# Mixer B: one of four chunks of the depth by seven block products instead of eight, in six pairs of projection column blocks

## The chip, the cores and the metric

The kernel runs on one core of a Trainium2 chip. The time is the device time of one execution in microseconds (us); less is better. Three runs of the kernel before gave 2266.64, 2268.15 and 2270.43 us, with a median of 2268.15 us. A core has five engines that work side by side: PE (TensorE, the matrix multiplier; the loading of its weights is shown as PEld), DVE (VectorE), ACT (ScalarE), POOL (GpSimd) and SP, whose queue starts most transfers. Each takes its own instructions strictly in the order in which they were written into its queue.

## The reference, cut to what matters

A trunk of two layers over 256 positions of width 2048, all in float32: attention A and a gated MLP, then attention B (mixer B) and a second gated MLP. The change is in mixer B:

```python
def mixer_b(h, w_qkv, w_o, rel_bias):
    qkv = (h @ w_qkv).reshape(b, s, 3, 3, 8, 128)     # groups g, q/k/v, heads
    for g, (window, dil) in enumerate(((128, 1), (512, 4), (2048, 16))):
        o, lz = dilated_group(qkv[:, :, g, 0], qkv[:, :, g, 1], qkv[:, :, g, 2], ...)
    wts = jax.nn.softmax(jnp.stack(log_zs, axis=0), axis=0)
    y = jnp.concatenate([wts[g][..., None] * outs[g] for g in range(3)], axis=2)
    return y.reshape(b, s, 3072) @ w_o
```

The product that matters is `h @ w_qkv`: 256 positions, a depth of 2048, and 9216 columns.

## The kernel before, in words

**One float32 product is three passes.** A weight block is loaded to SBUF (tile `raw`, 128 x 1024, which is 256 rows of depth by 512 columns, 512 KB), ACT copies it to a rounded tile `wh`, and DVE writes the rest `raw - wh` into `wl` (`split_raw`, L125). The positions are split in the same way into `xh` and `xl`. A product is then xh·wh, xh·wl and xl·wh, summed in a PSUM bank. For one block PE does 12 matmuls of 128 x 512: three passes, two halves of the depth, two halves `m` of the positions. Such a block of 12 matmuls is called a full block below.

**Rings.** `raw` has six buffers (`new_raw`), and `wh`/`wl` have three (`new_hl`; a fourth only in the down projections of the MLP). So the split of a block waits until PE has finished the block three before it. A split is issued with a priority (AHEAD = 45) that puts it ahead of other work in the queues of ACT and DVE.

**Mixer B** (`mixer_b`, L917) takes the heads in two halves `hf`. In each half it projects nine column blocks of 512 one after another: k and q of group 0, k and q of group 1, k and q of group 2, then v of groups 0, 1 and 2. A projection (`project`, L180) goes through four chunks `kg` of the depth with two full blocks each, so eight full blocks. It accumulates in two of the PSUM banks 0 to 3, and the next projection takes the other two. Banks 4 to 7 rotate through `ps_tile` and hold the small products of the attention.

**What runs beside the projections.** After a projection a generator is started: `k_gen` and `s_gen` copy the result from PSUM with a scale (L686, ACT), transpose 32 x 32 blocks (L335, DVE), and put the blocks in their places with 16 copies of 32 x 256 (L345 to L349: 12 on ACT, 4 on POOL). This gives kT and qT. Then `s_gen` makes the scores of four heads on PE (L305 for groups 1 and 2, L307 to L309 for group 0), adds the bias and takes the maximum (L975, L977, DVE) and the exponential (L986, ACT). A score matmul needs all 16 copies of qT. `v_gen` scales the probabilities (L1014, DVE), transposes them on PE (L1016), and multiplies them with v. `step()` moves the oldest waiting generator forward by one `yield`; it is called after each weight block. So the number of blocks between the end of a projection and a step of its generator is set by the code, and a scheduler then lays the instructions down in each engine's queue.

**Seven products.** The down projections of the MLP use `project_pair` (L215) already: two column blocks n0 and n1 are done together, and on chosen chunks the 2 x 2 x 2 block products (depth halves, position halves, column blocks) are done by seven instead of eight. A product P takes 6 matmuls, needs sums of positions (`forms`) and sums of weight blocks, which DVE adds in place in `raw` (L242), and leaves common terms M1, M5, M6 and M7 that are added to the four results afterwards (`combine`).

## Time and profile before

| | |
|---|---|
| median of three runs | 2268.15 us |
| the profiled execution | 2266.05 us, of which the span on the core is 2264.2 us |
| PE busy | 2248.7 us (99%) |
| DVE busy | 1635.8 us (72%) |
| ACT busy | 1504.0 us (66%) |
| mean granted TensorE clock | 0.998 |

The profile shows one execution. Times in it are counted from the start of the span. The end of a matmul in it is modelled, so that neighbouring matmuls overlap in the rows; the distance from start to start is what a matmul takes on PE. The projections of mixer B lie from 983.6 to about 1398 us; one projection with the attention work between its matmuls takes about 23 us.

### The profile page before, as it was taken

What the parts mean: (1) busy time and instruction counts of PE and PEld (TensorE: products, weight loads), DVE (VectorE), ACT (ScalarE), POOL (GpSimd) and SP (SyncE); (2) the same over time, 40 slices, a digit from 0 to 9 for tenths busy, and PEclk for the clock granted to TensorE, in tenths of its full rate; (3) what the DMA queues carried; (4) which work ended last, traced back from release to release, by engine and by line L of the source; (5) the groups of instructions that cost most, each with busy time, mean ns of one, the idle gap of its engine ahead of it and who ended that gap; (6) DMA issues with size and microseconds to landing.
All of it is one profiled execution on the core that took longest, in us unless ns stands there. A gap on an engine that the chain in (4) does not pass through costs nothing.

```text
span 2264.2 us, 28877 instructions
## 1 busy us (share of the span) xinstructions
PE 2248.7 (99%) x10169; PEld 1861.7 (82%) x10169; DVE 1635.8 (72%) x2213; ACT 1504.0 (66%) x2330; POOL 252.8 (11%) x372
## 2 busy tenths in 40 slices
PE   9999999999999999999999999999999999999998
PEld 7788888888888888888888888888888888888886
DVE  6776687888878778756565556465888788687784
ACT  6665776777547777767755774565777755577763
POOL 2210112200001010111100100000101100001110
PEclk9999999999999999999999999999999999999999
DMA  8444667756665655666555565566666656556763
GB/s 299 156 149 150 193 197 227 224 190 192 210 202 189 198 189 187 219 206 205 190 172 177 177 194 161 181 193 189 198 191 194 205 184 218 187 192 195 223 198 128
DMA packets 126449, 437.42 MB, mean 193 GB/s; under 512 B 17264, under 2 KB 18032, under 8 KB 126304
## 3 DMA queue, kind: packets, MB, share of 16 engines
q1 hardware_dynamic: 119744, 425.64, 58.2%
q0 software_dynamic: 6128, 9.38, 1.6%
q8 instruction: 79, 1.29, 0.2%
q10 hardware_dynamic: 432, 0.56, 0.1%
q14 instruction: 66, 0.54, 0.1%
HBM read 429.20 MB, written 6.29 MB: 192 GB/s over the span
## 4 chain that ended last, share of the span: by engine, by line
PE 96%; ACT 1%; DVE 1%; issue 1%; DMA 1%; POOL 0%; SPq 0%; POOLq 0%; DVEq 0%; ACTq 0%
PE acc L154 26%; PE acc L155 26%; PE acc L153 26%; PE acc L273 5%; PE acc L275 5%; PE acc L278 5%; PE ps L305 1%; PE ps L309 1%; PE ps L308 1%; PE ps L307 0%; DVE wl L129 0%; PE ps L868 0%; ACT tM L347 0%; ACT wh L128 0%; PE ps L1016 0%
## 5 line engine op out<-in xcount | busy, mean ns | idle before, releaser
L129 DVE TENSOR_TENSOR wl<-raw,wh 128x1024 fp32r<-128x1024 f32 x822 | 1009.0, 1233 | 478.2 <-ACT wh L128 475.8
L128 ACT ACTIVATE wh<-raw 128x1024 fp32r<-128x1024 f32 x822 | 867.3, 1058 | 550.1 <-PE acc L155 338.6
L153 PE MATMUL acc<-wh,xh 128*128 128x512 f32 x2176 | 851.9, 392 | 0.2 <-ACT wh L164 0.2
L154 PE MATMUL acc<-wl,xh 128*128 128x512 f32 x2176 | 848.4, 390 | 2.9 <-DVE wl L129 1.4
L155 PE MATMUL acc<-wh,xh 128*128 128x512 f32 x2176 | 847.5, 389 | 0.0
L154 PEld LDWEIGHTS acc<-wl,xh 128*128 128x128 f32 x2176 | 408.7, 188 | 89.9 <-DVE wl L129 5.5
L155 PEld LDWEIGHTS acc<-wh,xh 128*128 128x128 f32 x2176 | 408.5, 188 | 84.8
L153 PEld LDWEIGHTS acc<-wh,xh 128*128 128x128 f32 x2176 | 408.7, 188 | 83.4 <-ACT wh L164 0.6
L345 POOL COPY u<-t 32x256 f32<-32x256 f32 x176 | 110.7, 629 | 1039.9 <-DVE t L455 1031.8
L273 PE MATMUL acc<-wh,ah 128*128 128x512 f32 x524 | 204.1, 389 | 0.3 <-DVE h L408 0.3
L275 PE MATMUL acc<-wh,al 128*128 128x512 f32 x524 | 203.9, 389 | 0.0
L154 PE MATMUL acc<-wl,ah 128*128 128x512 f32 x480 | 187.0, 390 | 0.5 <-DVE wl L129 0.5
L153 PE MATMUL acc<-wh,ah 128*128 128x512 f32 x480 | 187.4, 390 | 0.0
L155 PE MATMUL acc<-wh,al 128*128 128x512 f32 x480 | 186.9, 389 | 0.0
L347 ACT ACTIVATE u<-t 32x256 f32<-32x256 f32 x352 | 147.8, 420 | 12.5 <-DVE t L455 4.6
L278 PE MATMUL acc<-wl,ah 128*128 128x512 f32 x524 | 146.0, 389 | 0.0
L273 PEld LDWEIGHTS acc<-wh,ah 128*128 128x128 f32 x524 | 98.4, 188 | 21.3 <-DVE h L408 1.0
L278 PEld LDWEIGHTS acc<-wl,ah 128*128 128x128 f32 x524 | 98.4, 188 | 20.4
L275 PEld LDWEIGHTS acc<-wh,al 128*128 128x128 f32 x524 | 98.4, 188 | 20.3
L154 PEld LDWEIGHTS acc<-wl,ah 128*128 128x128 f32 x480 | 90.2, 188 | 19.3 <-DVE wl L129 0.9
L155 PEld LDWEIGHTS acc<-wh,al 128*128 128x128 f32 x480 | 90.1, 188 | 18.7
L153 PEld LDWEIGHTS acc<-wh,ah 128*128 128x128 f32 x480 | 90.2, 188 | 18.1
(180 smaller groups left out, 1641.6 us busy)
## 6 DMA issues: line engine op xcount, KB each, us to landing
raw<-in_w_up_dram SPq DMA_DIRECT2D x352, 512.0 KB, 4.4
raw<-in_w_down_dram SPq DMA_DIRECT2D x176, 512.0 KB, 4.7
raw<-in_w_b_dram SPq DMA_DIRECT2D x144, 512.0 KB, 4.1
raw<-in_w_bo_dram SPq DMA_DIRECT2D x48, 512.0 KB, 4.1
raw<-in_w_a_dram SPq DMA_DIRECT2D x40, 512.0 KB, 4.7
raw<-in_w_ao_dram SPq DMA_DIRECT2D x32, 512.0 KB, 4.0
raw<-in_w_a_dram SPq DMA_DIRECT2D x16, 256.0 KB, 6.2
h<-in_x_dram SPq DMA_DIRECT2D x4, 512.0 KB, 8.9
```

Source lines behind the costliest of these rows:

```text
L128: nc.scalar.activation(wh, r, AF.Copy)
L129: nc.vector.tensor_tensor(wl, r, wh.bitcast(F32), ALU.subtract)
L153: nc.tensor.matmul(accs[m], xh, wh[:, j, :], start=st, stop=False)
L154: nc.tensor.matmul(accs[m], xh, wl[:, j, :], start=False, stop=False)
L155: nc.tensor.matmul(accs[m], xl, wh[:, j, :], start=False, stop=sp)
L273: nc.tensor.matmul(acc[k], xh, wh[:, j, :], start=k in fresh, stop=False)
L275: nc.tensor.matmul(acc[k], xl, wh[:, j, :], start=False, stop=False)
L278: nc.tensor.matmul(acc[k], xh, wl[:, j, :], start=False, stop=last[k] == i and j == 1)
L305: nc.tensor.matmul(o, lh[ls], rh[rs], start=start, stop=stop)
L308: nc.tensor.matmul(o, lh[ls], rl[rs], start=False, stop=False)
L345: nc.gpsimd.tensor_copy(dst, src)
L347: nc.scalar.activation(dst, src, AF.Copy)
```

## The change

In each half of the heads, k and q of group 0 are projected as before. The other projections, but for v of group 2, are taken in pairs through `project_pair`: k and q of group 1, k and q of group 2, and v of group 0 with v of group 1. That makes six pairs in all. In each pair the chunks 0 to 2 are 12 full blocks ("c", 12 matmuls each), and chunk 3 is done by seven products ("P", 6 matmuls each) where it was four full blocks (eight products). The order in a pair, by the list `units` of `seven`, is c P1 c P2 c c P5 c P3 c c P7 c P6 c P4 c c c. The first six c belong to the first column block, the last six to the second. The first block is complete after P4, the second three full blocks later.

The four results of a pair hold all four PSUM banks 0 to 3. M1, M5, M7 and M6 go through the rotating banks 4 to 7. ACT copies M1, M5 and M7 into SBUF (L1110), and DVE works out the four sums (L1112 to L1115). The results are then added to them in SBUF by DVE (L1118, L1119 for the first block, L1128, L1129 for the second), and k_gen, s_gen and v_gen read them from there. In each pair ACT and DVE split 19 blocks in place of 16, and DVE adds four pairs of weight blocks (L245). The sums of positions for chunk 3 are made once, by `last_forms`, at the end of the first MLP.

```diff
-    def project_pair(w, n0, n1, lhs, forms, units, late, early_done, n0_done):
+    def project_pair(w, n0, n1, lhs, forms, units, late, early_done, n0_done, product_done=None):
         home = {1: "M1", 2: "C11", 3: "C12", 4: "C21", 5: "M5", 6: "M6", 7: "M7"}
-        place = ("M1", "M5", "M6", "M7", "C11", "C21", "C12", "C22")
-        b = bank_at[0]
-        acc = {k: bank((4, 5, 6, 7, 2 - b, 3 - b, b, b + 1)[i], "acc") for i, k in enumerate(place)}
+        if product_done:
+            acc = dict(zip(("C11", "C21", "C12", "C22"), new_acc() + new_acc()))
+        else:
+            place = ("M1", "M5", "M6", "M7", "C11", "C21", "C12", "C22")
+            b = bank_at[0]
+            acc = {k: bank((4, 5, 6, 7, 2 - b, 3 - b, b, b + 1)[i], "acc") for i, k in enumerate(place)}
 
...
+            for k, *_ in todo:
+                if k not in acc:
+                    acc[k] = ps_tile()
...
+            if product_done and kind == "P" and home[p][0] == "M":
+                product_done(home[p], acc.pop(home[p]))
             if i == last_s:
                 early_done(acc)
-            if i == last["C21"]:
+            if i == max(last["C11"], last["C21"]):
                 n0_done(acc)
...
+    def last_forms(hT, turn_pair, n, g):
+        fm = hT["forms"] = {f: new_hT(4 * n + i)[:2] for i, f in enumerate((1, 0, 2, 4))}
+        for i, f in enumerate((7, 5, 6, 3)):
+            fm[f] = tuple(hpool.tile([P, NT], F32R, tag=f"al{k}", name=nm("sf")) for k in
+                          ((12, 13), (14, 15), (20, 21), (22, 23))[i])
+        for kt in range(4):
+            hT[4 * n + kt] = [tuple(t[:, kt % 2 * P:(kt % 2 + 1) * P] for t in fm[f])
+                              for f in ((1, 0), (2, 4))[kt // 2]]
+
+        def scaled(kp):
+            t = turn_pair(kp)
+            for j in range(2):
+                kt = 4 * n + 2 * kp + j
+                nc.scalar.activation(t[:, j * NT:(j + 1) * NT], t[:, j * NT:(j + 1) * NT], AF.Copy,
+                                     scale=gain[:, g, kt:kt + 1])
+            return t.rearrange("p (a t) -> p a t", a=2)
+
+        def put(f, src):
+            split(*(t.rearrange("p (a t) -> p a t", a=2) for t in fm[f]), src)
+
+        def tmp(k):
+            return hpool.tile([P, NT], F32, tag=f"ah{k}", name=nm("st")).rearrange("p (a t) -> p a t", a=2)
+
+        c0 = scaled(0)
+        put(1, c0[:, :, :P])
+        put(0, c0[:, :, P:])
+        yield
+        c1 = scaled(1)
+        put(2, c1[:, :, :P])
+        put(4, c1[:, :, P:])
+        x0, s1, s2, s3, s4 = (tmp(k) for k in (12, 13, 14, 15, 20))
+        yield
+        nc.scalar.activation(x0, c0[:, :, P:], AF.Copy)
+        nc.vector.tensor_tensor(s3, c0[:, :, :P], x0, ALU.subtract)
+        nc.vector.tensor_tensor(s1, c1[:, :, P:], x0, ALU.subtract)
+        put(7, s3)
+        put(5, s1)
+        yield
+        nc.vector.scalar_tensor_tensor(s2, s1, -1.0, c0[:, :, :P], ALU.mult, ALU.subtract)
+        nc.vector.tensor_tensor(s4, c1[:, :, :P], s2, ALU.add)
+        put(6, s2)
+        put(3, s4)
...
+                kTs = {}
+
+                def k_gen(g, accs, kTs=kTs):
                     ks = evac_scaled(bp, accs, rstd)
                     yield
                     yield
+                    kT = kTs[g] = pair_tile(bp, [P, 4, NT], "kT", 1, g > 0)
                     yield from heads_T_dve(kT, ks, bp, "vl")
 
-                def s_gen(g, accs, kT, bts, nmx=nmx, lsum=lsum, nmv=nmv, probs=probs, e=e):
+                def s_gen(g, accs, bts, nmx=nmx, lsum=lsum, nmv=nmv, probs=probs, e=e, kTs=kTs):
                     qs = evac_scaled(bp, accs, rstd)
-                    qT = pair_tile(bp, [P, 4, NT], "qT", 1, g > 0)
-                    yield
-                    yield
+                    yield
+                    yield
+                    kT, qT = kTs[g], pair_tile(bp, [P, 4, NT], "qT", 1, g > 0)
                     yield from heads_T_dve(qT, qs, bp, "vl")
...
                 def v_gen(g, accs, hf=hf, probs=probs, e=e):
+                    if g > 0:
+                        yield
                     v = evac_split(bp, accs, rstd, g > 0)
...
+                def seven(n0, n1, sums, n0_ready, n1_ready):
+                    (k0, k1), (q0, q1) = sums
+                    chores = []
+
+                    def product_done(k, t):
+                        if k != "M6":
+                            nc.scalar.activation({"M1": k0, "M5": q1, "M7": k1}[k], t, AF.Copy)
+                            return
+                        nc.vector.tensor_tensor(q0, t, k0, ALU.add)
+                        nc.vector.tensor_tensor(k1, k1, q0, ALU.add)
+                        nc.vector.tensor_tensor(q0, q0, q1, ALU.add)
+                        nc.vector.tensor_tensor(q1, k1, q1, ALU.add)
+
+                    def n0_done(a):
+                        nc.vector.tensor_tensor(k0, a["C11"], k0, ALU.add)
+                        nc.vector.tensor_tensor(k1, a["C21"], k1, ALU.add)
+                        n0_ready([k0, k1])
+
+                    cs = [("c", k, i) for i2 in range(2) for k in kgs[:3] for i in (2 * i2, 2 * i2 + 1)]
+                    units = [cs.pop(0)]
+                    for p, c in zip(ORDER, (1, 2, 1, 2, 1, 1, 3)):
+                        units += [("P", 3, p)] + [cs.pop(0) for _ in range(c)]
+                    a = project_pair(w_b, n0, n1, hT, {3: hT["forms"]}, units, None, lambda a: None,
+                                     n0_done, product_done)
+                    nc.vector.tensor_tensor(q0, a["C12"], q0, ALU.subtract)
+                    nc.vector.tensor_tensor(q1, a["C22"], q1, ALU.subtract)
+                    n1_ready([q0, q1])
+
                 for g in range(3):
                     bts = biases(hf, g)
-                    ka = project(w_b, 6 * g + 2 + hf, hT, kgs)
-                    kT = pair_tile(bp, [P, 4, NT], "kT", 1, g > 0)
-                    start(k_gen(ka, kT))
-                    start(s_gen(g, project(w_b, 6 * g + hf, hT, kgs), kT, bts))
-                for g in range(3):
-                    start(v_gen(g, project(w_b, 6 * g + 4 + hf, hT, kgs)))
+                    n0, n1 = 6 * g + 2 + hf, 6 * g + hf
+                    if g == 0:
+                        start(k_gen(g, project(w_b, n0, hT, kgs)))
+                        start(s_gen(g, project(w_b, n1, hT, kgs), bts))
+                    else:
+                        sums = [[bp.tile([P, 512], F32, tag=t, name=nm("ms"), bufs=2) for _ in range(2)]
+                                for t in ("pTh", "pTl")]
+                        seven(n0, n1, sums, lambda a: start(k_gen(g, a)), lambda a: start(s_gen(g, a, bts)))
+                sums = [(lambda t: [t[:, 0], t[:, 1]])(bp.tile([P, 2, 512], F32, tag=t, name=nm("ms"), bufs=1))
+                        for t in ("kTl", "qTl")]
+                seven(4 + hf, 10 + hf, sums, lambda a: start(v_gen(0, a)), lambda a: start(v_gen(1, a)))
+                start(v_gen(2, project(w_b, 16 + hf, hT, kgs)))
```

How the queues change shows at three places. In the rows, `wh` and `wl` are the split of a weight block, `stg` is the copy of a projection's result, `tT` its transposed blocks, `ms` an SBUF tile that holds one of the four sums of a pair, `acc` a result bank and `ps` a rotating bank.

The first place is ACT's queue from the copies of the q projection (k and q of group 1, first half of the heads) to the last copies that place qT. Before:

```order
L686 ACTIVATE stg_9566<-acc_9387,rstd_8814 128x512
L128 ACTIVATE wh_9616<-raw_9612 128x1024
L686 ACTIVATE stg_9566<-acc_9388,rstd_8814 128x512
L128 ACTIVATE wh_9648<-raw_9613 128x1024
L347 ACTIVATE qT_9569<-tT_9609 32x8x32 x6
L128 ACTIVATE wh_9668<-raw_9664 128x1024
L347 ACTIVATE qT_9569<-tT_9609 32x8x32 x6
L128 ACTIVATE wh_9684<-raw_9665 128x1024
```

And in the changed kernel, where ten copies of kT of the same group stand in the row ahead of these:

```order
L128 ACTIVATE wh_9675<-raw_9673 128x1024
L355 ACTIVATE kT_9567<-tT_9568 32x8x32 x2
L745 ACTIVATE stg_9625<-ms_9204,rstd_8814 128x512
L745 ACTIVATE stg_9625<-ms_9205,rstd_8814 128x512
L128 ACTIVATE wh_9709<-raw_9707 128x1024
L128 ACTIVATE wh_9721<-raw_9719 128x1024
L1110 ACTIVATE ms_9629<-ps_9661 128x512
L355 ACTIVATE qT_9669<-tT_9670 32x8x32
L128 ACTIVATE wh_9742<-raw_9737 128x1024
L355 ACTIVATE qT_9669<-tT_9670 32x8x32 x8
L128 ACTIVATE wh_9767<-raw_9655 128x1024
L355 ACTIVATE qT_9669<-tT_9670 32x8x32 x3
```

Before, the 12 copies of kT are long done when q is copied, and three splits stand between the first copy of q and the end of qT. Now the copies of kT stand just ahead of the two copies of q, four splits and a copy of M1 stand between those and the end of qT, and q is read from `ms` after DVE has finished it. On PE the first score matmul of the group stands six weight blocks behind the end of the q projection in both kernels; before all six are full blocks, now four are full blocks and two are products.

The second place is DVE's queue at the end of a pair (the same k and q). Before, at the end of the k projection and behind it:

```order
L335 STREAM_TRANSPOSE tT_9439<-stg_9384 128x512 x2
L975 SCALAR_TENSOR_TENSOR lg_9416<-ps_9409,bt_8818 128x512
L129 TENSOR_TENSOR wl_9479<-raw_9443,wh_9478 128x1024
L977 TENSOR_REDUCE nmx_8821<-lg_9416 128x2
L129 TENSOR_TENSOR wl_9499<-raw_9494,wh_9498 128x1024
L129 TENSOR_TENSOR wl_9515<-raw_9495,wh_9514 128x1024
L129 TENSOR_TENSOR wl_9535<-raw_9530,wh_9534 128x1024
L129 TENSOR_TENSOR wl_9551<-raw_9531,wh_9550 128x1024
L129 TENSOR_TENSOR wl_9578<-raw_9573,wh_9577 128x1024
L129 TENSOR_TENSOR wl_9594<-raw_9574,wh_9593 128x1024
L335 STREAM_TRANSPOSE tT_9609<-stg_9566 128x512
```

And in the changed kernel from the four sums to the second half of k's transposition:

```order
L1112 TENSOR_TENSOR ms_9204<-ps_9504,ms_9202 128x512
L129 TENSOR_TENSOR wl_9552<-raw_9549,wh_9551 128x1024
L1113 TENSOR_TENSOR ms_9203<-ms_9203,ms_9204 128x512
L1118 TENSOR_TENSOR ms_9202<-acc_9206,ms_9202 128x512
L129 TENSOR_TENSOR wl_9574<-raw_9571,wh_9573 128x1024
L1114 TENSOR_TENSOR ms_9204<-ms_9204,ms_9205 128x512
L343 STREAM_TRANSPOSE tT_9568<-stg_9546 128x512
L1115 TENSOR_TENSOR ms_9205<-ms_9203,ms_9205 128x512
L129 TENSOR_TENSOR wl_9608<-raw_9605,wh_9607 128x1024
L1119 TENSOR_TENSOR ms_9203<-acc_9207,ms_9203 128x512
L129 TENSOR_TENSOR wl_9640<-raw_9637,wh_9639 128x1024
L343 STREAM_TRANSPOSE tT_9568<-stg_9546 128x512
```

The transposition of k stands behind the sums of the pair, the two additions of the first column block and four splits; before it waited for nothing but the copy of k and the splits.

The third place is DVE's queue around v of group 0 (first half of the heads), whose first product with the probabilities needs `vh`, `vl` and `pTl` (`pr` are probabilities, `pT` their transposition). Before:

```order
L297 SCALAR_TENSOR_TENSOR vl_10138<-acc_9945,rstd_8814,vh_10137 128x512
L975 SCALAR_TENSOR_TENSOR lg_10131<-ps_10128,btg_8820 128x2x128
L297 SCALAR_TENSOR_TENSOR vl_10138<-acc_9946,rstd_8814,vh_10137 128x512
L977 TENSOR_REDUCE nmx_8821<-lg_10131 128x2
L129 TENSOR_TENSOR wl_10216<-raw_10211,wh_10215 128x1024
L975 SCALAR_TENSOR_TENSOR lg_10168<-ps_10165,btg_8820 128x2x128
L977 TENSOR_REDUCE nmx_8821<-lg_10168 128x2
L129 TENSOR_TENSOR wl_10254<-raw_10212,wh_10253 128x1024
L993 TENSOR_TENSOR mn_10174<-mn_10174,nmx_8821 128x8
L994 TENSOR_TENSOR e_8823<-mn_10174,nmx_8821 128x24
L996 TENSOR_TENSOR lsum_8822<-lsum_8822,e_8823 128x24
L997 TENSOR_TENSOR mn_10174<-lsum_8822 128x8
```

And in the changed kernel, from the last split ahead of the first column block's addition:

```order
L129 TENSOR_TENSOR wl_10370<-raw_10367,wh_10369 128x1024
L1113 TENSOR_TENSOR ms_10032<-ms_10032,ms_10033 128x512
L1118 TENSOR_TENSOR ms_10032<-acc_10034,ms_10032 128x512
L1114 TENSOR_TENSOR ms_10033<-ms_10033 128x512
L129 TENSOR_TENSOR wl_10399<-raw_10396,wh_10398 128x1024
L1115 TENSOR_TENSOR ms_10033<-ms_10032,ms_10033 128x512
L305 SCALAR_TENSOR_TENSOR vl_10362<-ms_10032,rstd_8814,vh_10361 128x512
L1119 TENSOR_TENSOR ms_10032<-acc_10035,ms_10032 128x512
L129 TENSOR_TENSOR wl_10439<-raw_10436,wh_10438 128x1024
L305 SCALAR_TENSOR_TENSOR vl_10362<-ms_10032,rstd_8814,vh_10361 128x512
L299 TENSOR_TENSOR pTl_10393<-ps_10385,pTh_10392 128x512
```

Before, `vl` was written with the scores of group 2 still running (at 1142.92 and 1143.92 us; the first `pTl` at 1152.03 us). Now both halves of `vl` stand behind the sums of the pair, and `pTl` stands directly behind them.

11 lines of the change are left out of this document (8 added, 3 removed).

## The prediction

> **What bounds the kernel now.** I read the page first, then PE's waits, then mixer B by windows, then the order of time around one q projection.
>
> ```profile
> span 2264.2 us, 28877 instructions
> ...
> PE 2248.7 (99%) x10169; PEld 1861.7 (82%) x10169; DVE 1635.8 (72%) x2213; ACT 1504.0 (66%) x2330; POOL 252.8 (11%) x372
> ...
> PE 96%; ACT 1%; DVE 1%; issue 1%; DMA 1%; POOL 0%; SPq 0%; POOLq 0%; DVEq 0%; ACTq 0%
> ```
>
> PE is busy 99% of the span and is 96% of the chain that ended last. Its waits for other engines, all of them:
>
> ```profile
> PE acc L154 <- DVE wl L129: 1.9, 4, 0.8
> PE ps L396 <- DVE warm L393: 1.5, 1, 1.5
> PE acc L154 <- DVE wl L165: 1.1, 1, 1.1
> PE ps L309 <- DVE qTl L291: 0.6, 1, 0.6
> PE acc L273 <- DVE h L408: 0.3, 1, 0.3
> PE acc L153 <- ACT wh L164: 0.2, 1, 0.2
> ```
>
> That is 5.6 us. So each matmul removed is worth its full distance to the next one, and each wait that arises is paid in full. The other engines in the down projections with seven products (855 to 910), in mixer B, in one k and q projection of it (1074 to 1119.4), and where its softmax ends:
>
> ```profile
> core 0: us, PE busy (x) PEld busy (x) DVE busy (x) ACT busy (x) POOL busy (x), PEclk, DMA share, GB/s
> 855.00:910.00 55.00, 55.00 (x245) 45.54 (x244) 48.59 (x65) 40.63 (x59) 5.16 (x8) 1.00 0.59 191
> 1074.00:1119.40 45.40, 45.40 (x210) 37.86 (x209) 25.72 (x30) 32.76 (x60) 5.77 (x9) 1.00 0.60 191
> 1140.00:1163.00 23.00, 22.89 (x122) 19.23 (x121) 21.07 (x52) 14.10 (x29) 0.75 (x1) 1.00 0.52 171
> 983.60:1398.00 414.40, 414.17 (x1951) 345.68 (x1950) 245.91 (x324) 270.63 (x462) 41.31 (x61) 1.00 0.59 187
> ```
>
> **What it removes.** Six pairs lose one product of 6 matmuls each: 36. The busy time of one is modelled, so I take starts:
>
> ```profile
> 955.05 0.39 PE L153 MATMUL acc<-wh,ah 128*128 128x512 f32 x1
> ...
> 983.38 0.39 PE L155 MATMUL acc<-wh,al 128*128 128x512 f32 x1
> ```
>
> Between these two lie 125 steps: 28.33 / 125 = 0.2266 us. So a full block is 2.72 us, a product 1.36 us, and the gain is 36 x 0.2266 = 8.2 us, if PE never waits.
>
> **What it adds, and what covers it.**
>
> ```profile
> L128 ACT ACTIVATE wh<-raw 128x1024 fp32r<-128x1024 f32 x822 | 867.3, 1058 | 550.1 <-PE acc L155 338.6
> L129 DVE TENSOR_TENSOR wl<-raw,wh 128x1024 fp32r<-128x1024 f32 x822 | 1009.0, 1233 | 478.2 <-ACT wh L128 475.8
> L242 DVE TENSOR_TENSOR raw<-raw,raw 128x1024 f32<-128x1024 f32 x40 | 49.0, 1225 | 11.3 <-DMA raw<-in_w_down_dram 11.0
> L628 DVE TENSOR_TENSOR cu<-acc,cu 128x512 f32<-128x512 f32 x6 | 4.1, 689 | 0.0
> L625 ACT ACTIVATE cu<-acc 128x512 f32<-128x512 f32 x6 | 3.5, 579 | 0.0
> raw<-in_w_b_dram SPq DMA_DIRECT2D x144, 512.0 KB, 4.1
> ```
>
> Per pair DVE gets 3 more splits (3.7), 4 weight additions (4.9) and 8 additions of results (5.5): 14.1 us. With the 25.7 of the window that is 39.8 in 45.4 - 1.4 = 44.0 us, 90%. ACT gets 3 x 1.06 + 3 x 0.58 = 4.9, so 37.7, 86%. The down projections ran with DVE at 88% and PE at 55.00 of 55.00, so on average the work fits; I charge nothing for it, and with the cover gone the four weight additions come out, 4.9 us a pair. The forms (`last_forms`) add some 9 copies and 8 subtractions of about 0.42 us beside the first k projection, which needs them only at its seventh block: nothing, at most 3.7 us. Bytes and loads stay the same; from P5 to P7 four of six raw buffers are held, so the load of c7 starts only after the split of c5, but lands 4.1 us later and c7 follows c5 by 6.8 us on PE: nothing. The results hold four banks; the first column block's are read 3 us before the next pair writes them: nothing.
>
> **What it moves: place one, qT between pairs (four times).** The score matmul of a group stands six blocks behind the end of its q projection. That was 6 x 2.72 = 16.3 us and becomes 4 x 2.72 + 2 x 1.36 = 13.6 us. What must happen in that time, before:
>
> ```profile
> 1119.44 0.69 ACT L686 ACTIVATE stg<-acc,rstd 128x512 f32<-128x512 f32 x1 [0.98 <-PE acc L155]
> 1123.93 2.55 ACT L347 ACTIVATE qT<-tT 32x256 f32<-32x256 f32 x6
> 1127.59 2.54 ACT L347 ACTIVATE qT<-tT 32x256 f32<-32x256 f32 x6
> 1130.16 2.01 ACT L128 ACTIVATE wh<-raw 128x1024 fp32r<-128x1024 f32 x2
> 1131.25 2.36 DVE L129 TENSOR_TENSOR wl<-raw,wh 128x1024 fp32r<-128x1024 f32 x2 [2.43 <-ACT wh L128]
> 1136.24 0.60 PE L305 MATMUL ps<-kT,qT 128*128 128x128 f32 x4
> ```
>
> The copies of qT end at 1130.13, 10.7 us after q's copy began; the scores start at 1136.24, with 6.1 us to spare. A copy of 32 x 256 takes 2.55 / 6 = 0.425 us in a row, a split on DVE 2.36 - 1.23 = 1.13 when another follows; for a 128 x 512 operation followed by another I take 0.61:
>
> ```profile
> 1152.03 0.68 DVE L291 TENSOR_TENSOR pTl<-ps,pTh 128x512 fp32r<-128x512 f32 x1
> 1152.63 1.13 DVE L1014 TENSOR_SCALAR pr<-pr,e 128x256 f32<-128x256 f32 x4
> ```
>
> Now the new queue, from the end of P6 on PE (0). PE goes c 2.7, P4 4.1, three c 12.2, then the next pair's c P1 c P2 c c to 25.8, where the scores stand. DVE is at 0.9 (split of P4, for whose buffer it waited) and must do four splits and eight smaller operations in the order shown before k's second transposition ends: 0.9 + 4 x 1.13 + 8 x 0.63 = 10.5. ACT then places ten copies of kT (4.25, at 14.8), a split (15.9), two copies (16.8), the two copies of q, ready since 13.6 (18.0), two splits (20.0), M1 (20.5), one copy of qT, a split, eight, a split, three (27.8). So the scores wait 27.8 - 25.8 = 2.0 us. The spare 6.1 went to 2.7 for the shorter blocks, 1.4 for DVE's additions of the second block, and 4.2 for kT's copies ahead of q. Bounds: nothing, if ACT were as in the rows above (10.7 + 1.4 is under 13.6), and 4.5 us if all 12 copies of kT (5.1) came behind a ready q. I take 2.0, four times: 8.0 us.
>
> **Place two, group 0 into the first pair (twice).**
>
> ```profile
> 1027.60 0.69 ACT L686 ACTIVATE stg<-acc,rstd 128x512 f32<-128x512 f32 x1 [0.98 <-PE acc L155]
> ...
> 1039.28 1.04 ACT L290 ACTIVATE qTh<-stg 128x1024 fp32r<-128x1024 f32 x1
> ...
> 1040.55 1.22 DVE L291 TENSOR_TENSOR qTl<-stg,qTh 128x1024 fp32r<-128x1024 f32 x1
> ```
>
> Before, qTh was there 12.7 us and qTl 14.2 us after q's copy began. Now the budget is 13.6; added in ACT's queue are M1 (0.5), one split and in DVE's queue a weight addition (1.1) ahead of the second transposition: qTh at 15.3, qTl at 16.7. The first score waits 1.7, its third pass 0.5 more: 2.2 us, twice 4.4. Bounds: 0 (qTh unmoved at 12.7) and 3.3 (both splits of P5 and c4 behind the copies, 2.1 + 1.2).
>
> **Place three, v of group 0 (twice).** The scores of group 2, the softmax and eight scalings fell beside blocks of 2.72 us; the window at 1140 shows DVE at 21.07 of 23.00. Now DVE gets two weight additions there, reaches the four sums some 3 us late, and `pTl` stands behind them, 3 splits, five 0.61 operations and two `vl`: 3.1 + 3.4 + 3.1 + 2.0 + 0.6 = 12.2 us after P6. PE is there after 10.4. About 1.8 us, twice 3.6. Bounds: 0 and 3.7, with one more split and hops between ACT and DVE.
>
> **Sum.** -8.2 + 8.0 + 4.4 + 3.6 = +7.8 us. The profiled execution took 2266.05 us, below the lowest of the three runs (2266.64), 2.1 us below their median. 2266.05 + 7.8 = 2273.9; by the median 2276.0. I give 2275.
>
> **A wait and the clock.** The warm-up at the start ran slowly:
>
> ```profile
> 1.46 4.15 PE L396 MATMUL ps<-warm 128*128 128x512 f32 x11 [1.46 <-DVE warm L393]
> ```
>
> (4.15 - 0.55) / 10 = 0.36 us from start to start with 0.55 for the last, against 0.227 later. If each new wait let PE fall back to that pace for eleven matmuls, it would cost 11 x 0.13 = 1.5 us more at eight places: +12, 2286 us. [...]
>
> **Rivals.**
> - *All hidden, faster.* If kT's copies begin 2 us earlier (at 8.5 instead of 10.5), qT ends at 25.8 and place one is free; it decides whether DVE clears its queue after P6 in 7.6 us rather than 9.6. With the other two places free too: 2275 - 16.0 = 2259. For it: the down projections hide the same products without a wait. Against: no score waits for them there. 0.10.
> - *Even.* The waits come to about half: 2267. 0.20.
> - *DVE becomes the bound.* Behind P5 up to P4 three weight additions and the logits meet nine splits; if 1.2 us per addition reach PE, three in each pair, that is 3 x 1.2 x 6 = 22 more at most, half of it likely: 2286. For it: 90%; against: 88% ran free, with four split buffers there and three here. 0.14.
> - *The clock falls back* as above: 2286. 0.04.
>
> My forecast, the waits at the three places at 12 to 21 us, 2270 to 2280: 0.52.
>
> **How the numbers follow.** About 0.2% (4.5 us) is what can be told from no change. Faster is the first rival: 0.10. Same is the even case and the low end of the forecast (under 2272.7): 0.20 + 0.04. Slower is the rest: 0.66. The range reaches from between the first two rivals, 2263, to above the DVE rival, 2288; the forecast's own is 2270 to 2280.
>
> **What would show it.** Right: PE's waits have new rows, scores (L313, L315) on ACT's copies (L355) or on qTh and qTl of about 2 us each, six in all, and L315/L316 on `pTl` or `vh`; the distance of two q ends and the matmul count (36 fewer) as given. Wrong: no such rows (first rival); long rows of L284 on `wl` or L279 on `wh` in the pairs (DVE or ACT as the bound); a granted clock under 0.99.

## The result and the profile after

The changed kernel takes 2274.65 us in the median of ten runs (2270.00 to 2278.60), the kernel before 2267.43 us beside it (2265.34 to 2270.43). The ratio is 1.0031, with a 95% interval of 1.0022 to 1.0039: slower by 0.3%. The prediction was 2275 us, with the mechanism of waits at three places. The mechanism and the total hold. The sizes of the terms do not, and one term was missing.

The page of the changed kernel, in its first part:

```profile
span 2274.0 us, 28978 instructions
...
PE 2246.9 (99%) x10133; PEld 1856.4 (82%) x10133; DVE 1712.0 (75%) x2311; ACT 1531.4 (67%) x2375; POOL 261.9 (12%) x372
```

The 36 matmuls are gone (10169 became 10133), and PE's busy time fell by only 1.8 us where 8.2 us of work went away. PE's waits for other engines, all of them:

```profile
PE ps L313 <- issue: 4.8, 4, 1.2
PE ps L315 <- ACT qTh L298: 3.6, 2, 1.9
PE acc L154 <- DVE wl L129: 2.6, 5, 0.8
PE ps L316 <- DVE pTl L299: 1.5, 2, 0.8
PE ps L317 <- DVE qTl L299: 1.5, 3, 0.6
PE ps L455 <- DVE warm L452: 1.5, 1, 1.5
PE acc L279 <- DVE h L467: 1.4, 2, 0.7
PE acc L154 <- DVE wl L165: 0.5, 1, 0.5
PE acc L153 <- ACT wh L164: 0.3, 1, 0.3
```

17.7 us stand where 5.6 us stood before. The new rows are the three places: four scores on L313 (place one; the view gives "issue" for them, but they start just behind the last copy of qT, below), two on `qTh` and two of the three on `qTl` (place two), two on `pTl` (place three). Almost the whole loss lies in one stage. From the first matmul of mixer B's projections to the first of its output projection it was 983.61 to 1408.28, 424.67 us. Now it is 984.40 to 1418.10, 433.70 us:

```profile
984.40 0.39 PE L153 MATMUL acc<-wh,xh 128*128 128x512 f32 x1
...
1418.10 0.48 PE L153 MATMUL acc<-wh,ah 128*128 128x512 f32 x1
```

That is 9.03 us more. The profiled execution took 2275.74 us, 9.69 more than the one before, so 0.66 us lie elsewhere. The medians differ by less, by 7.2 us. Below, "the stage" is this stretch, and a loss "by starts" is the time from the start of one matmul to the start of the next, less 0.2266 us for 512 columns. For 256 and 128 columns I take 0.1133 and 0.0567, an estimate in proportion; in a row, in the kernel before, six matmuls of 256 columns stand 0.12 us apart and four of 128 take 0.37 us up to the next start. A loss by starts can be larger than the idle time in the wait rows, since the view lets a matmul run on for a while.

Place one, ScalarE in the second pair of the first half, and the score that waits:

```profile
1075.74 4.26 ACT L355 ACTIVATE kT<-tT 32x256 f32<-32x256 f32 x10
1080.02 1.06 ACT L128 ACTIVATE wh<-raw 128x1024 fp32r<-128x1024 f32 x1
1081.11 0.84 ACT L355 ACTIVATE kT<-tT 32x256 f32<-32x256 f32 x2
1081.98 1.34 ACT L745 ACTIVATE stg<-ms,rstd 128x512 f32<-128x512 f32 x2
...
1090.68 1.06 ACT L128 ACTIVATE wh<-raw 128x1024 fp32r<-128x1024 f32 x1
1091.77 1.26 ACT L355 ACTIVATE qT<-tT 32x256 f32<-32x256 f32 x3
...
1093.13 0.68 PE L313 MATMUL ps<-kT,qT 128*128 128x128 f32 x4 [1.25 <-issue]
```

All twelve copies of kT stand ahead of q's two scaled copies, in the trace as in the queue. The last copy of qT ends at 1093.03, and the score starts at 1093.13. By starts the four scores lose 1.41, 1.32, 1.38 and 1.32 us.

Something else appears in the windows. In each row stand the busy time and the count of PE, its weight loads, VectorE, ScalarE and GpSimd, then the granted clock of TensorE, the DMA share and GB/s:

```profile
1042.25:1045.66 3.41, 1.58 (x7) 0.72 (x5) 3.25 (x3) 2.98 (x4) 0.00 (x0) 1.00 0.01 5
1045.66:1049.08 3.42, 3.11 (x11) 2.83 (x12) 3.24 (x5) 1.43 (x2) 0.00 (x0) 0.50 0.49 158
1049.08:1052.50 3.42, 3.42 (x20) 2.94 (x19) 3.42 (x5) 3.40 (x8) 0.00 (x0) 1.00 0.51 162
...
1260.70:1264.11 3.41, 1.33 (x6) 0.86 (x7) 3.41 (x4) 2.53 (x3) 0.00 (x0) 1.00 0.06 10
1264.11:1267.53 3.42, 3.42 (x14) 3.13 (x15) 3.34 (x4) 1.55 (x2) 0.00 (x0) 0.50 0.40 144
```

Behind both waits of place two the clock is halved for 3.42 us. PE counts as busy there, so no row of the waits shows it. From 1045.97 to 1049.11 start 1.59 us worth of matmuls (eight of 256 columns, three of 512), so this stretch costs 1.55 us. In the other PE has no gap: 3.42 us at half the clock lose 1.7 us.

The stage adds up by starts: place one 5.4, place two 1.85 + 0.61 and 2.11 + 0.61 = 5.2, place three 1.05 twice = 2.1, the two slow stretches 3.3, together 16.0. Less the 8.2 of the matmuls that is + 7.8 of the + 9.0 us. The other 1.2 us are in gaps of 0.3 us and less around small matmuls, which I cannot assign.

### The profile page after: what moved, and what is told of

Same layout as the page of the kernel before. It is cut to its first block, busy times and chain, and to the rows that moved or that the text cites. A ratio compares the mean times of both kernels' runs of the same rounds, so it can differ in the third digit from the quotient of the medians.

```text
span 2274.0 us, 28978 instructions
## 1 busy us (share of the span) xinstructions
PE 2246.9 (99%) x10133; PEld 1856.4 (82%) x10133; DVE 1712.0 (75%) x2311; ACT 1531.4 (67%) x2375; POOL 261.9 (12%) x372
## 3 DMA queue, kind: packets, MB, share of 16 engines
q8 instruction: 79, 1.29, 0.2%
## 4 chain that ended last, share of the span: by engine, by line
PE 76%; DVE 3%; ACT 1%; issue 1%; DMA 1%; POOL 0%; DVEq 0%; POOLq 0%; ACTq 0%
PE acc L154 17%; PE acc L153 17%; PE acc L155 17%; PE acc L279 7%; PE acc L281 7%; PE acc L284 7%; DVE wl L129 1%; DMA scr<-lnt 1%; ACT wh L128 1%; PE ps L313 0%; DMA raw<-in_w_b_dram 0%; DVE pr L1078 0%; ACT qT L355 0%; PE ps L281 0%; PE ps L284 0%
## 5 line engine op out<-in xcount | busy, mean ns | idle before, releaser
L129 DVE TENSOR_TENSOR wl<-raw,wh 128x1024 fp32r<-128x1024 f32 x840 | 1030.7, 1233 | 410.4 <-ACT wh L128 406.9
L128 ACT ACTIVATE wh<-raw 128x1024 fp32r<-128x1024 f32 x840 | 884.3, 1057 | 526.7 <-PE acc L155 291.8
L154 PE MATMUL acc<-wl,xh 128*128 128x512 f32 x1792 | 698.7, 390 | 2.9 <-DVE wl L129 2.1
L153 PE MATMUL acc<-wh,xh 128*128 128x512 f32 x1792 | 700.6, 391 | 0.3 <-ACT wh L164 0.3
L155 PE MATMUL acc<-wh,xh 128*128 128x512 f32 x1792 | 697.9, 389 | 0.0
L154 PEld LDWEIGHTS acc<-wl,xh 128*128 128x128 f32 x1792 | 336.5, 188 | 75.1 <-DVE wl L129 5.3
L155 PEld LDWEIGHTS acc<-wh,xh 128*128 128x128 f32 x1792 | 336.4, 188 | 70.2
L153 PEld LDWEIGHTS acc<-wh,xh 128*128 128x128 f32 x1792 | 336.4, 188 | 69.6 <-ACT wh L164 0.7
L279 PE MATMUL acc<-wh,ah 128*128 128x512 f32 x524 | 204.1, 389 | 1.4 <-DVE h L467 1.4
L284 PE MATMUL acc<-wl,ah 128*128 128x512 f32 x524 | 146.1, 389 | 0.0
L279 PE MATMUL acc<-wh,xh 128*128 128x512 f32 x312 | 122.5, 393 | 0.0
L281 PE MATMUL acc<-wh,xh 128*128 128x512 f32 x312 | 121.5, 390 | 0.0
L279 PEld LDWEIGHTS acc<-wh,ah 128*128 128x128 f32 x524 | 98.3, 188 | 22.6 <-DVE h L467 2.2
L284 PEld LDWEIGHTS acc<-wl,ah 128*128 128x128 f32 x524 | 98.3, 188 | 20.5
L281 PEld LDWEIGHTS acc<-wh,al 128*128 128x128 f32 x524 | 98.4, 188 | 20.4
```

The lines of the kernel that those rows point to most:

```text
L128: nc.scalar.activation(wh, r, AF.Copy)
L129: nc.vector.tensor_tensor(wl, r, wh.bitcast(F32), ALU.subtract)
L153: nc.tensor.matmul(accs[m], xh, wh[:, j, :], start=st, stop=False)
L154: nc.tensor.matmul(accs[m], xh, wl[:, j, :], start=False, stop=False)
L155: nc.tensor.matmul(accs[m], xl, wh[:, j, :], start=False, stop=sp)
L279: nc.tensor.matmul(acc[k], xh, wh[:, j, :], start=k in fresh, stop=False)
```

## The experiments

All times are medians, with the kernel before run beside each. "Stage" is the length of the stage in the one profiled execution.

| kernel | us | ratio to before, 95% | stage, us |
|---|---|---|---|
| before | 2267.43 | | 424.67 |
| changed | 2274.65 | 1.0031 (1.0022 to 1.0039) | 433.70 |
| scores of groups 1, 2 later | 2276.72 | 1.0036 (1.0024 to 1.0049) | 430.93 |
| scores of group 0 later | 2270.21 | 1.0013 (1.0004 to 1.0022) | 427.58 |
| scores of groups 1, 2 earlier | 2287.95 | 1.0087 (1.0061 to 1.0112) | 440.05 |
| filled wait | 2271.80 | 1.0017 (1.0006 to 1.0028) | 430.11 |
| v of group 0 alone | 2271.47 | 1.0017 (1.0008 to 1.0026) | 426.40 |
| kT on GpSimd | 2267.70 | 1.0002 (0.9993 to 1.0010) | 423.40 |
| v of group 0 alone, all scores later | 2270.20 | 1.0014 (1.0005 to 1.0022) | 426.26 |
| v of group 0 alone, kT on GpSimd, group 0 later | 2264.34 | 0.9986 (0.9977 to 0.9995) | 419.50 |
| kT on GpSimd, group 0 later | 2265.55 | 0.9987 (0.9978 to 0.9996) | 420.61 |
| the same, first product with v later | 2264.29 | 0.9981 (0.9972 to 0.9990) | 421.05 |
| before, with kT on GpSimd | 2268.08 | 1.0002 (0.9993 to 1.0011) | 424.68 |
| kT on GpSimd, group 0 later, v plain | 2264.24 | 0.9980 (0.9971 to 0.9988) | 422.41 |

A profiled execution can hold a long wait in another stage: in three of them an MLP waited 3.1 to 3.7 us for one weight block. In each of the three, and in one more, the clock was also halved for 3.4 us there. So stages are compared by the trace, and kernels by their medians. The kernels ran in five sets, and the median of the kernel before lay from 2266.92 to 2267.98 us in them, so a difference of a microsecond between two rows says little.

**Is the clock's fall caused by the wait?** The wait stays and is filled with work that nobody needs.

```diff
                         s = ps_tile()
+                        for d in range(16 if g == 0 and i == 0 else 0):
+                            nc.tensor.matmul(s[:, :NT], hT[0][0][:, :P], hT[0][0], start=True, stop=True)
```

> Sixteen matmuls of 128 x 256 that nobody needs stand ahead of the first score of group 0, into the bank that this score then overwrites: 16 x 0.1133 = 1.8 us of TensorE work in the stretch in which it waits for qTh (1.85 and 2.11 us). The order of the scheduler also moves by a row or two there. Theory (the clock falls because TensorE did too little in the 3.4 us before; the two stretches end on the same grid of 3.4133 us, 64 steps apart): with the gap filled the clock stays at 1.00, the work itself costs nothing, and the kernel gets faster by 2.9 us: 2271.8 us, 2270.5 to 2273. Rival (the clock falls for another reason, or TensorE pays for the added work): 2274.6 to 2278, with the stretches of 0.50 as before.

Measured: 2271.80 us, 2.85 less than the changed kernel, with 32 matmuls more. PE at the first place, then two windows at each place:

```profile
1043.69 2.08 PE L1031 MATMUL ps<-xh 128*128 128x256 f32 x16
1045.60 0.28 PE L315 MATMUL ps<-kTh,qTh 128*128 128x256 f32 x1
1045.72 0.28 PE L316 MATMUL ps<-kTl,qTh 128*128 128x256 f32 x1
1046.30 0.39 PE L317 MATMUL ps<-kTh,qTl 128*128 128x256 f32 x1 [0.30 <-DVE qTl L299]
```

```profile
1041.00:1046.00 5.00, 5.00 (x31) 4.33 (x29) 3.34 (x3) 4.93 (x9) 0.00 (x0) 1.00 0.34 114
1046.00:1049.40 3.40, 3.10 (x19) 2.80 (x19) 3.37 (x4) 2.08 (x3) 0.00 (x0) 1.00 0.20 52
1259.00:1262.50 3.50, 3.50 (x27) 3.27 (x26) 2.97 (x3) 3.34 (x4) 0.00 (x0) 1.00 0.04 13
1262.50:1266.00 3.50, 3.50 (x22) 3.07 (x21) 3.47 (x5) 1.54 (x2) 0.00 (x0) 1.00 0.43 136
```

The useless matmuls take the place of the wait, and the clock stays at 1.00 behind them. Here no 3.41 us, wherever they begin, hold less than 3.1 us of PE work; in the changed kernel the emptiest hold 1.2. That part of the loss comes from too little work on PE. The scheduler also put one split on VectorE behind `qTl` instead of ahead of it. The stage's gain of 3.6 us holds 0.3 more than the clock's 3.3, and that may come from there. By the medians the case is weaker: 2.85 us less, or 2.3 by the distances from the kernel before beside each, and the two intervals overlap.

**The waits of group 0 taken away.**

```diff
+                    if g == 0:
+                        yield
+                        yield
                     for i in range(4):
                         yield
                         s = ps_tile()
```

> The scores of group 0 stand two units later (a product of 1.36 us and a block of 2.72 us), those of groups 1 and 2 as in the changed kernel. In that kernel the first of group 0 loses 1.85 + 0.61 and 2.11 + 0.61 us, 5.2 in all, and after each of these two places the granted clock reads 0.50 for some 3.4 us, which by starts costs about 1.45 us more each. Theory (both the waits and the slow stretches come from the one cause, that qTh and qTl are late): all of it goes, 2274.65 - 5.2 - 2.9 = 2266.5 us, 2265.5 to 2268.5, and no stretch of 0.50 is left between 984 and 1418. Rival (the slow clock has a cause of its own): 2269 to 2270, with the stretches still there. Second rival (ScalarE and VectorE are the bound): 2273 to 2276.

Measured: 2270.21 us, 4.4 less; the stage is 6.1 us shorter. Both waits and both slow stretches are gone: the clock is 1.00 in both places.

```profile
1044.00:1060.00 16.00, 16.00 (x81) 13.55 (x80) 14.12 (x15) 12.96 (x20) 0.00 (x0) 1.00 0.50 166
1262.00:1278.00 16.00, 16.00 (x83) 13.69 (x82) 14.96 (x16) 11.30 (x21) 0.00 (x0) 1.00 0.55 171
```

The expectation of 2266.5 us was missed by 3.7. Part of the reason is that waits come back in the next pair, on `wl` and `wh`:

```profile
PE acc L284 <- DVE wl L129: 1.0, 3, 0.6
PE acc L279 <- ACT wh L128: 0.4, 2, 0.3
```

In the first half they stand at 1086 and 1087 us, over 20 us behind the last logits of group 0 (1063.3 us). So those logits are not what is ahead of them; what makes these splits late is not shown.

**Place one: later scores, earlier scores.**

```diff
+                    if g > 0:
+                        yield
                     for i in range(4):
```

> The scores of groups 1 and 2 stand one unit later on TensorE (behind the product of 1.36 us that now follows the first of them); nothing else moves. In the changed kernel the first of them waits 1.41, 1.32, 1.38 and 1.32 us by starts (1.25, 1.16, 1.22 and 1.16 in the rows of the waits). Theory (the scores stand too early by about what the blocks became shorter, and the other engines have time to spare): the four rows on L313 fall to 0.1 us or vanish, and the kernel takes 2274.65 - 5.4 = 2269.2 us, 2268 to 2271. Rival (ScalarE and VectorE are the bound, at 90% of the time): the waits come back at other places, on wh, wl or the logits, and the time stays at 2273 to 2276.

Measured: 2276.72 us, nothing gained (the stage of its profiled execution, without a slow stretch, is 2.8 us shorter; the median does not show it). The rows on L313 did go, but others came:

```profile
PE ps L1082 <- DVE pr L1080: 3.7, 2, 2.0
PE acc L279 <- ACT wh L128: 2.3, 6, 0.6
```

L1082 is the transposes of group 0's probabilities: place three. The logits of group 2 moved back into a stretch in which VectorE had 24.39 of 32 us to do in the kernel before, and 30.67 in the changed one (the same window of each):

```profile
1143.00:1175.00 32.00, 31.89 (x163) 26.74 (x163) 24.39 (x55) 17.39 (x30) 0.75 (x1) 1.00 0.51 163
```

```profile
1143.00:1175.00 32.00, 31.14 (x152) 25.83 (x151) 30.67 (x55) 19.53 (x37) 0.75 (x1) 1.00 0.72 232
```

So to move the consumer was no cure; the rival's time came out here, 0.7 us above its range.

```diff
                     for i in range(4):
-                        yield
+                        if i or g == 0:
+                            yield
```

> The scores of groups 1 and 2 stand one unit earlier, ahead of a block of 2.72 us: the opposite dose. Theory: qT's copies keep their place on ScalarE, so each of the four waits grows by the 2.72 us of the block, to some 4.1 us: + 10.9. If a gap of that length also halves the clock for 3.4 us, as it did behind the waits of group 0, four times about 1.5 more: 2274.65 + 10.9 + 6 = 2291.5 us, 2288 to 2294, with four more stretches of 0.50; if the clock stays, 2285.5. Rival (the other engines are the bound, and where TensorE waits does not matter): 2274 to 2279.

Measured: 2287.95 us, 13.3 more, in two runs only. The four waits by starts are 3.00, 2.93, 3.01 and 2.90, not 4.1. The growth is 1.6 us and not 2.72, because the block that now follows the score leaves its split of 1.06 us behind the copies of qT too. The clock fell behind two of the four waits, and at one of them for 6.83 us. For these four waits and the two of group 0 (the first and the fourth row), each row is a window of 3.41 us that ends where the clock fell or, where it did not fall, at a distance from the falls that is a whole multiple of 3.4133 us (an estimate from the distances between falls, which stand at the end):

```profile
1048.32:1051.73 3.41, 1.61 (x8) 1.14 (x9) 3.41 (x4) 2.25 (x3) 0.00 (x0) 1.00 0.16 46
1092.69:1096.10 3.41, 2.00 (x9) 1.31 (x7) 1.23 (x1) 3.30 (x9) 1.52 (x2) 1.00 0.53 174
...
1140.48:1143.89 3.41, 1.49 (x7) 0.91 (x5) 0.99 (x2) 3.32 (x9) 0.98 (x1) 1.00 0.73 219
...
1266.78:1270.19 3.41, 1.66 (x8) 0.88 (x6) 2.99 (x3) 3.23 (x4) 0.00 (x0) 1.00 0.02 8
1311.15:1314.56 3.41, 1.42 (x7) 0.85 (x5) 1.02 (x2) 3.32 (x9) 0.99 (x1) 1.00 0.75 226
1362.35:1365.76 3.41, 0.68 (x5) 0.35 (x4) 1.22 (x1) 3.30 (x9) 0.00 (x0) 1.00 0.74 238
```

It fell behind the first, the fifth and the sixth, not behind the second, the third and the fourth.

**The cause of place one: kT's copies.**

```diff
-                    yield from heads_T_dve(kT, ks, bp, "vl")
+                    yield from heads_T_dve(kT, ks, bp, "vl", "ppaa" if g else "paaa")
```

Each letter stands for four of the 16 blocks: `p` places them on GpSimd, `a` on ScalarE. (The helpers that pass the string on are left out.)

> For groups 1 and 2, GpSimd places 8 of the 16 blocks of kT instead of 4, ScalarE 8 instead of 12; nothing stands elsewhere in TensorE's order. Theory (the copies of kT ahead of q in ScalarE's queue make qT late: ten of them ran from 1075.74 to 1080.00 while the sums of q had been ready since 1079.07, and the first copy of q began at 1081.98): four copies less are 4 x 0.425 = 1.7 us, more than the waits of 1.3 to 1.4 us: the four rows on L313 go, 2274.65 - 5.4 = 2269.2 us, 2268 to 2271. Rival (ScalarE fills the time with splits, or GpSimd's copies of 1.3 us beside VectorE make kT late): at most half goes, 2272 to 2276.

Measured: 2267.70 us, 6.95 less, and the stage 10.3 us shorter. No row on L313 is left. ScalarE and the score, to be set beside the rows of the changed kernel above, and GpSimd:

```profile
1073.89 2.98 ACT L355 ACTIVATE kT<-tT 32x256 f32<-32x256 f32 x7
...
1078.41 1.34 ACT L745 ACTIVATE stg<-ms,rstd 128x512 f32<-128x512 f32 x2
...
1087.91 1.70 ACT L355 ACTIVATE qT<-tT 32x256 f32<-32x256 f32 x4
...
1089.79 0.60 PE L313 MATMUL ps<-kT,qT 128*128 128x128 f32 x4
```

```profile
1073.77 4.33 POOL L353 COPY kT<-tT 32x256 f32<-32x256 f32 x8 [14.06 <-DVE tT L343]
1080.61 4.40 POOL L353 COPY qT<-tT 32x256 f32<-32x256 f32 x4 [2.51 <-DVE tT L343]
```

q's scaled copies begin 4.5 us behind the first copy of kT where it was 6.2, and the score waits for nothing. The four copies taken off ScalarE, 1.7 us, cover the wait of 1.4: with the order of the work on PE unchanged, this settles the cause. The stage gained 4.9 us more than the four waits. 3.3 of that are the slow stretches, which this execution does not have although `qTh` still came late (what may lie behind that stands at the end); 1.0 is a shorter second wait of group 0.

```diff
 # in the kernel before the change
-                    yield from heads_T_dve(kT, ks, bp, "vl")
+                    yield from heads_T_dve(kT, ks, bp, "vl", "paaa" if kT[1] else "ppaa")
```

> The kernel before the change with GpSimd placing 8 of the 16 blocks of kT for groups 1 and 2. Its scores waited for no copy. Theory (the edit pays only because the change made qT late): no difference, 2267.1 us, 2266 to 2268.2. Rival (less work on ScalarE pays in itself): 2260 to 2264.

Measured: 2268.08 us against 2267.83 beside it, no difference. The edit is worth nothing where qT is not late.

**Place three: can v of group 0 be helped?** Three tries, by order.

```diff
-                seven(4 + hf, 10 + hf, sums, lambda a: start(v_gen(0, a)), lambda a: start(v_gen(1, a)))
-                start(v_gen(2, project(w_b, 16 + hf, hT, kgs)))
+                start(v_gen(0, project(w_b, 4 + hf, hT, kgs)))
+                seven(10 + hf, 16 + hf, sums, lambda a: start(v_gen(1, a)), lambda a: start(v_gen(2, a)))
```

(The line that makes `sums` stands between the two new ones.)

> Of v, group 0 is projected alone and first, and groups 1 and 2 by seven products (before: groups 0 and 1 by seven, 2 alone). The number of matmuls stays. Softmax, scaling and the scores of group 2 then fall beside plain blocks of 2.72 us, as in the kernel before the change. Theory (place three: VectorE is behind there because the weight additions and sums of the v pair meet the logits, the scalings and the splits of v of group 0): the two waits on pTl, 1.05 us each by starts, go; 2274.65 - 2.1 = 2272.5 us, 2271 to 2273.5; all other waits stay. Rival (the low half of group 0 needs VectorE so much that it comes late wherever a pair stands): new waits on pTl, vl or pr in the pair that now follows, 2274.5 to 2278.

Measured: 2271.47 us, 3.2 less. The rows on `pTl` went, but the transposes now wait for the scaling, as the rival had it:

```profile
PE ps L1080 <- DVE pr L1078: 3.3, 2, 1.8
```

The stage became 7.3 us shorter in this execution and the output projection behind it 1.9 us longer (135.4 for 133.5 us). In it two of the four rows on L313 are missing and the clock shows no 0.50, so the trace credits the order of v with what is not its own.

> Group 0 of v alone and first; the scores of group 0 two units later, those of groups 1 and 2 one unit later. With only the latter the waits of place one had gone, but VectorE, which had no idle time from 1143 to 1175, scaled the probabilities of group 0 so late that their transposes waited 2.0 and 2.2 us. Theory (each wait stands where a consumer is early on TensorE, and with v of group 0 beside plain blocks there is room for all of them): places one, two and three and the two slow stretches go, 2274.65 - 5.4 - 5.2 - 2.9 - 2.1 = 2259.0 us, 2258 to 2263, faster than before the change by 0.2 to 0.4%. Rival (VectorE is short of time over the whole stretch, so that waits come back on wl, wh or the logits): 2265 to 2270.

Measured: 2270.20 us, the rival, 0.2 above its range. (Of the 32 us from 1143 to 1175 VectorE was busy for 30.19 in the kernel with later scores, so "no idle time" was too strong.) The waits on the scaling stay, 3.3 us, and 1.4 us on `wh` come with the later scores.

> Group 0 of v alone and first, the scores of group 0 two units later, and GpSimd placing 8 of the 16 blocks of kT for groups 1 and 2, whose scores stay where the changed kernel has them. It removes the same waits in another way, with less left for ScalarE and the logits not moved back. Theory: 2274.65 - 5.4 - 5.2 - 2.9 - 2.1 = 2259.0 us, 2258 to 2263. Rival (VectorE is short of time over the whole stretch): 2265 to 2270.

Measured: 2264.34 us, 10.3 less than the changed kernel and 0.14% faster than before. Not the 2259 of the theory: 3.1 us of waits stay, and the output projection is 2.0 us longer.

**The two edits that paid, together, and with a later product.** With v as the change has it:

> The changed kernel, v in its order, with the two edits that paid by themselves: GpSimd places 8 of the 16 blocks of kT for groups 1 and 2 (2267.70 us alone), and the scores of group 0 stand two units later (2270.21 alone). Theory (the two places are independent): 2274.65 - 6.95 - 4.44 = 2263.3 us, 2261 to 2264.5, with the two waits on pTl of 1.05 us as the only ones over 1 us left in the projections of mixer B. Rival (with the logits of group 0 two units later, splits come late, as the rows on wl and wh of 1.4 us in the kernel with that edit alone): 2265 to 2267.5.

Measured: 2265.55 us, at the rival's end, though no row on wl or wh is left in the stage: 1.5 us on `pTl` and 1.3 us on L313 are all. The profiled execution (2260.70 us) was the fastest of its eleven. What the others lost is not shown.

```diff
                     for k in range(5):
                         yield
+                        if k == 1 and g == 0:
+                            yield
```

> As the kernel with both edits, and the first product of probabilities and v of group 0 stands one unit more behind its transpose. Theory (place three: TensorE comes 1.05 us too early for pTl, twice, and VectorE catches up in one unit): 2.1 us less than that kernel, 2261.2 us by its expectation, 2259 to 2262.5. Rival (VectorE had no idle time there from 1143 to 1175, so that the wait only moves to the following products or transposes, on pr, vl or pTl): the same time as that kernel within 1 us.

Measured: 2264.29 us, 1.3 less, within the runs' spread. The wait moved, to the low half of the output of the product before (and the waits on L313 stand at 2.4 us, where they were 1.3):

```profile
PE ps L315 <- DVE al L299: 2.1, 2, 1.2
```

So in the same stretch VectorE is late wherever the products with v stand. That is the rival's mechanism; its time (within 1 us) was missed by 0.3.

```diff
-                seven(4 + hf, 10 + hf, sums, lambda a: start(v_gen(0, a)), lambda a: start(v_gen(1, a)))
-                start(v_gen(2, project(w_b, 16 + hf, hT, kgs)))
+                for g in range(3):
+                    start(v_gen(g, project(w_b, 6 * g + 4 + hf, hT, kgs)))
```

> The kernel with both edits that paid (8 blocks of kT on GpSimd, the scores of group 0 two units later; 2265.55 us), but all three groups of v projected alone, without products: 12 of the 36 matmuls come back, 12 x 0.2266 = + 2.7 us. Theory (the v pair costs its two waits on pTl, 1.04 us each, and nothing else): - 2.1 + 2.7 = + 0.6: 2266.2 us, 2265 to 2267.5, and no wait on pTl, pr or vl left. Rival (the v pair costs more than its waits, since VectorE has no idle time beside it): 2261 to 2264.

Measured: 2264.24 us, between the theory and the rival. No wait on `pTl`, `pr` or `vl` is left in the stage; two on L313 are, 1.7 us. By the stage of one execution each it is 1.8 us longer than with the v pair, by the medians 1.3 us faster, and the intervals overlap. Whether the v pair earns anything is left open; neither figure gives it its whole 2.7 us.

## Why the prediction was right, and where it was not

- **The gain, 8.2 us.** The count fell by 36. The gain is visible only where the waits are removed: with two edits the stage is 420.6 us, 4.1 under the kernel before.
- **Place one, "27.8 - 25.8 = 2.0 us", four times.** The mechanism is right in each step and shown by the run with kT on GpSimd. The size was 1.4. The trace has qT's end at 27.2 us from the end of P6 (1065.8) instead of 27.8, and the score's turn at 25.9. VectorE was sooner: k's second transposition ended at 9.7 and not at 10.5 (the sum there takes 0.63 us an operation, where the text ahead of it takes 0.61). So 5.4 us stand for the 8.0.
- **Place two, 2.2 us, twice.** It was 2.46 and 2.72, 5.2 us for the 4.4. `qTh` came 15.9 us after q's copy began (1028.39 to 1044.27), not 15.3, and `qTl` 17.5, not 16.7: one split more than I counted stood ahead.
- **Place three, "about 1.8 us", twice.** It was 1.05, 2.1 us for the 3.6. That VectorE is behind there is right, and firmer than I had it: each kernel that kept a v pair and moved work about there kept a wait, there or beside it.
- **The clock, 0.04 as a rival, nothing in the sum.** This step failed. That a wait of 2 us costs no more than its length is shown by no run. The two slow stretches of 1.55 and 1.7 us came behind waits of 1.7 to 1.95 us by the rows (1.85 and 2.11 by starts), followed by another of 0.61. It happened at two of the eight places, not at all of them as the rival had it. The end of the trace of the kernel before shows a fall as well. The last matmul starts at 2254.65 us, so PE is idle for some 2.1 us of the first window here and busy in the rest, and behind it the clock is halved:

```profile
2253.77:2257.18 3.41, 1.26 (x6) 0.72 (x4) 2.49 (x8) 1.95 (x3) 0.62 (x2) 1.00 0.26 94
2257.18:2260.59 3.41, 0.00 (x0) 0.00 (x0) 1.54 (x3) 0.72 (x1) 0.51 (x1) 0.50 0.94 351
```

- **"Charged nothing" for VectorE's average load.** True for the pairs of k and q, where no long row of L284 on `wl` or L279 on `wh` appeared. At place three it is the bound in fact, as the rival *DVE becomes the bound* said of all pairs.
- **The sum.** The predicted waits were 16.0 us, the measured ones 12.7. The clock (3.3), small gaps (1.2) and other stages (0.7) took the place of the difference, and more: 17.9 us less 8.2 is the 9.7 between the two profiled executions. The medians differ by 7.2, against the 7.8 of the forecast, so 2275 against 2274.65 is partly luck.

## What to carry to other kernels

When PE's blocks get shorter, count what the other engines must finish per block ahead of each consumer, in the order of their queues. The cure that worked took work out of the queue that was late; moving the consumer back paid for the scores of group 0, but at place one it pushed the followers into the next crowded stretch. A wait of two microseconds on PE can cost more than its length (here waits of 1.85 and 2.11 us by starts brought 1.55 and 1.7 us of lost clock), so look at the granted clock behind it before the wait is priced. Do not count on products saved in a stretch where VectorE has 1.3 us in 32 to spare: what the v pair earned here could not be told from nothing by the medians.

## What was not expected of the hardware

- **The clock fell behind windows in which PE was only partly idle.** It was halved for 3.42 us (once for 6.83) behind windows of 3.41 us in which PE was busy for 1.58 and 1.33 us in the changed kernel and for 1.61, 1.42 and 0.68 us in the run with earlier scores. In that run it stayed at 1.00 behind windows with 2.00, 1.66 and 1.49, so busy time alone (whose ends are modelled) does not draw the border. It also fell there at 399.79 us, behind a window in which PE was busy for 0.00 us. In these two traces the falls lie whole multiples of 3.4133 us apart, about the length of one slow stretch. In the trace of the changed kernel they stand at 1045.66, 1264.11 and, behind the last matmul (the rows below), 2267.63 us: 218.45 and 1003.52 us apart, 64 and 294 times 3.4133. In that of the run with earlier scores they stand at 399.79, 1051.73, 1314.56 and 1365.76 us: 191, 77 and 15 times.

```profile
2264.22:2267.63 3.41, 1.15 (x6) 0.61 (x4) 2.40 (x6) 1.95 (x3) 0.74 (x2) 1.00 0.29 108
2267.63:2271.04 3.41, 0.00 (x0) 0.00 (x0) 1.54 (x3) 0.72 (x1) 0.39 (x1) 0.50 0.94 351
```

- **The same wait had two prices.** Of the four waits of 2.9 to 3.0 us in the run with earlier scores two were followed by a slow stretch. The kernel with kT on GpSimd points at where the difference lies. Its first wait of group 0 is as long as in the changed kernel (1.92 + 0.61 us by starts), and the emptiest 3.41 us there, from 1042.08 on, hold 1.21 us of PE work. But its clock is halved at the end of the program at 2258.14. If its falls, too, stand only whole multiples of 3.4133 us apart (my estimate, from the distances above), the places near these waits are 355 and 293 steps earlier, at 1046.41 and 1258.03, and the windows that end there hold 2.12 and 2.02:

```profile
1043.00:1046.41 3.41, 2.12 (x11) 1.61 (x12) 3.41 (x4) 1.75 (x2) 0.00 (x0) 1.00 0.26 53
...
1254.62:1258.03 3.41, 2.02 (x9) 1.08 (x9) 3.41 (x4) 2.52 (x3) 0.00 (x0) 1.00 0.06 11
```

The clock stays at 1.00 behind both. Whether this spreads the ten executions of the changed kernel is not shown. The two with a mean granted clock of 0.999 took 2270.00 and 2270.75 us, the eight with 0.997 or 0.998 took 2273.80 to 2278.60. But a halving in any stage, and at the end of the program, enters that mean, and the kernel before has the same link without these waits: in one set its runs at 0.999 took 2265.59 to 2269.83 us, those at 0.997 took 2272.67 to 2274.91.

- **Useless work made the kernel faster.** 32 matmuls in the two waits kept the clock at 1.00, and the median fell by 2.85 us (with the doubt about that size given above).
- **GpSimd's copies came in two lengths.** In the run with kT on GpSimd eight copies of 32 x 256 took 4.33 us, 0.54 each in the mean, and four a little later 4.40 us, 1.10 each. In the stage of the changed kernel 26 single ones took 0.39 to 0.40 us and 22 took 1.29 to 1.46, with none between. Each of the 22 ran beside a split on VectorE (L129) for more than 1.0 us, none of the 26 for more than 0.34. So the trace points at the splits as what holds these copies up; no run tried it.
